# Token-major gate and up products, with the convolution's neighbour rows brought by DMA copies

## The chip, the cores and the metric

The kernel runs on one core of a Trainium2 chip. A core has TensorE (PE, matrix products; its weight loads are listed as PEld), VectorE (DVE), ScalarE (ACT), GpSimd (POOL) and SyncE (SP, which here only issues transfers), each with a queue of its own that it works through in order, and 16 DMA engines. SBUF is the on-chip memory of 128 partitions, PSUM the memory into which PE writes. The metric is the time on the device in microseconds (us); lower is better.

## The reference, cut to what matters

One layer over 256 tokens of width 2048: a normalised input goes through two token mixers, whose merged result is added to x; then comes a gated MLP with a causal convolution of three taps over the tokens, and a last normalisation. The change lies in the MLP (D_FF = 5632):

```python
h = rmsnorm(x, norm_ffn_w[l])
gate, up = jnp.split(jnp.einsum('bsd,df->bsf', h, w_up[l]), 2, axis=-1)
gate = causal_dwconv(gate, conv_ffn_w[l]) + conv_ffn_b[l]   # y[t] = g[t-2] w0 + g[t-1] w1 + g[t] w2
x = x + jnp.einsum('bsf,fd->bsd', jax.nn.gelu(gate, approximate=False) * up, w_down[l])
return rmsnorm(x, norm_final_w)
```

The convolution is taken for each of the 5632 channels alone, over the tokens. Everything is float32.

## The kernel before, in words

Products are formed from pairs of numbers: each float32 operand is split into a high part in the fp32r format and a low part, the rest. A product is hi·hi + lo·hi + hi·lo.

**Weights.** `srcs` lists all weights tiles in the order of use, 256 rows by 512 columns each, 512 KB. `begin` (L104) loads one on SP's queue into `raw` (four buffers, L109), ACT casts it to `whi` (L111), and DVE takes the rest as `wlo` (L118); `whi` and `wlo` have three buffers each. `weights()` keeps three tiles begun, the one in use and two ahead. A `raw` buffer is free for the next load when its `wlo` is made, a `whi` or `wlo` buffer when PE has used it.

**Two forms of a product.** `gemm_a` (L137) has the tokens on PSUM's partitions: for each of the two rows of 128 in a weights tile and each half of the tokens (t) it issues three matmuls of 512 columns (L148 to L150), twelve per tile; the stationary operand is a 128x128 block of the activations, the weights stream. Its result is `[128 tokens, 2, 512 channels]`, two PSUM banks from the pool `psm`, which has two such buffers. At the second tile it runs whatever waits in the list `later`. `gemm_b` (L156) has the channels on the partitions: the weights are stationary, and 512 columns stream past, the high part of all 256 tokens beside the low part (L172); a second matmul of 256 columns takes the weights' low part (L173). That is 16 matmuls per tile, and four results `[128 channels, 2, 256]` that come by turns from `psm` and from `psg` (four buffers of one bank). `merged` (L177) adds the two halves: ACT copies one out (L181), DVE adds (L182).

**The mixers** (to 777 us) use `gemm_a`; their results are evicted by ACT with the norm's factor as a scale (L449) and turned by `turned` (L185), eight transposes on PE against the identity (L193). One part of them (`gdn`) sends small matrices through DRAM: `cd` to `cdd`, `cdd` to `lb` (L553, L556), and DVE reads `lb` at L565.

**The MLP** (L794 to L823) has eleven chunks of 512 channels. Each has a gate product and an up product of eight weights tiles. The gate's result is merged, multiplied with the norm's factor `rb2` (one value per token, broadcast over the partitions at L303), and convolved: the tokens are on the free axis, so that a neighbour is a shifted slice (L804 and eight instructions at L808), with the taps as one value per partition (`cfw`, `vec`, turned at L268 and L278 at the kernel's start). Then come Gelu on ACT (L810), a multiplication with `rb2` on POOL (L811), the multiplication with the up product (L813), and the split in `hhi` and `hlo` (L820, L821), which are the stationary operands of the down projection.

**The down projection** (L841 to L850) holds its result in eight banks at once, four column groups (c) by two halves of the tokens, and goes through 22 pairs of rows; for each pair and c it takes one weights tile and twelve matmuls (L836 to L838).

**The order** on each queue is laid out when the program is built, by a planner that estimates how long each instruction and transfer takes and lets the earliest ready one go first; at run time each engine goes through its queue in that order and waits at an instruction until its inputs are there.

Of the kernel before, what the change touches and what calls it, by code (L numbers as in the profile page):

```python
# [7 lines left out]
F32 = mybir.dt.float32  # L8
# [5 lines left out]
P = 128  # L14
S = 256
# [7 lines left out]
PAD = 16  # L23
NB = 128 + PAD + 128
# [9 lines left out]
def kernel(  # L34
# [59 lines left out]
    srcs += [down[c][kp] for kp in range(KF // 2) for c in range(4)]  # L94
# [58 lines left out]

    banks = [0]

    def gemm_b(rhl, nk):  # L156

        banks[0] ^= 1  # L160
        if banks[0]:
            pair = [pm(), pm()]
            ps = [pair[f // 2][:, f % 2].rearrange("p (a s) -> p a s", a=2) for f in range(4)]
        else:
            ps = [pg([P, 2, S]) for f in range(4)]
        for c in range(nk // 2):
            hi, lo = weights()
            for f in range(4):
                fs = slice(f * P, (f + 1) * P)
                for kk in range(2):  # L170
                    k = 2 * c + kk
                    mm(ps[f], hi[:, kk, fs], rhl(k), start=(k == 0), stop=False, skip_group_check=True)  # L172
                    mm(ps[f][:, 1, :], lo[:, kk, fs], rhl(k)[:, 0, :], start=False, stop=(k == nk - 1),  # L173
                       skip_group_check=True)
        return ps

    def merged(ps, dst):  # L177

        for f in range(4):
            low_half = fp.tile([P, S], F32, tag="lh", bufs=3, name=nm("lh"))  # L180
            nc.scalar.copy(low_half, ps[f][:, 1, :])  # L181
            nc.vector.tensor_tensor(dst[:, f, :], ps[f][:, 0, :], low_half, op=ALU.add)  # L182
        return dst
# [66 lines left out]
    NV = 16 + KF  # L250
    V_FFN, V_CB = 0, 16
    vrows = mp.tile([NV, P], F32, tag="th", name="vrows")
    for off, n, src in ((V_FFN, 16, norm_ffn_w), (V_CB, KF, conv_ffn_b)):
        nc.scalar.dma_start(vrows[off : off + n, :], src[0].rearrange("(r p) -> r p", p=P))
    cqrows = mp.tile([96, 2, P], F32, tag="cy", bufs=2, name="cqrows")
    nc.scalar.dma_start(cqrows, conv_qkv_w.rearrange("o j (r p) -> (o j r) p", p=P)
                        .rearrange("(a q) p -> q a p", a=2))
    cfrows = mp.tile([66, 2, P], F32, tag="cy", bufs=2, name="cfrows")
    nc.scalar.dma_start(cfrows, conv_ffn_w.rearrange("o j (r p) -> (o j r) p", p=P)
# [6 lines left out]
    vec = cpool.tile([P, NV], F32, name="vec")  # L266
    pv = pg()
    nc.tensor.transpose(pv[:, :NV], vrows, ident[:NV, :NV])  # L268
    nc.vector.tensor_copy(vec, pv[:, :NV])
# [20 lines left out]
    def rstd_rows(ssq, dst):  # L290
# [6 lines left out]
        if dst is None:  # L297
            return rs
        pr = pg()
        for t in range(2):  # L300
            dg = cpool.tile([P, P], F32, tag="diag", bufs=2, name=nm("diag"))
            nc.vector.tensor_scalar(dg, ident, rs[:, t : t + 1], None, op0=ALU.mult)
            mm(pr[:, t * P : (t + 1) * P], ones, dg, start=True, stop=True)  # L303
        nc.vector.tensor_copy(dst, pr[:, :S])
        return rs
# [8 lines left out]
    rs1 = rstd_rows(ssq, None)  # L314
# [454 lines left out]
    for c in range(4):  # L769
        ps = gemm_a(at(mhi), at(mlo), KD)  # L770
        xs = xt[:, :, c * 512 : (c + 1) * 512]
        nc.vector.tensor_tensor(xs, xs, ps, op=ALU.add)
        for t in range(2):
            jk = cpool.tile([P, 512], F32, tag="sqj", name=nm("sqj"))
            nc.scalar.activation(jk, xs[:, t, :], AF.Square, accum_out=ssq4[:, t, c : c + 1])
        for k2 in range(2):
            pt = pg([P, 2, S])
            for kk in range(2):
                k = 4 * c + 2 * k2 + kk
                for t in range(2):  # L780
                    nc.tensor.transpose(pt[:, kk, t * P : (t + 1) * P], xt[:, t, k * P : (k + 1) * P], ident)
            for kk in range(2):
                k = 4 * c + 2 * k2 + kk
                nw = vec[:, V_FFN + k : V_FFN + k + 1]
# [11 lines left out]
    rb2b = rb2.unsqueeze(1).to_broadcast([P, 4, S])  # L796
    for c in range(DFF // 512):
        ps = gemm_b(lambda k: fhl[:, k], KD)
        gs = fp.tile([P, 4, S], F32, tag="gs", bufs=2, name=nm("gs"))
        nc.vector.tensor_tensor(gs, merged(ps, gs), rb2b, op=ALU.mult)  # L800
        y = fp.tile([P, 4, S], F32, tag="y", name=nm("y"))
        for f in range(4):
            r = 4 * c + f
            nc.vector.tensor_scalar(y[:, f, :], gs[:, f, :], cfw[:, 2 * KF + r : 2 * KF + r + 1],  # L804
                                    vec[:, V_CB + r : V_CB + r + 1], op0=ALU.mult, op1=ALU.add)
            for j in (1, 0):
                s = 2 - j
                nc.vector.scalar_tensor_tensor(y[:, f, s:], gs[:, f, : S - s], cfw[:, j * KF + r : j * KF + r + 1],  # L808
                                               y[:, f, s:], op0=ALU.mult, op1=ALU.add)
        nc.scalar.activation(y, y, AF.Gelu)  # L810
        nc.gpsimd.tensor_tensor(y, y, rb2b, op=ALU.mult)  # L811
# [15 lines left out]
    acc = [[pg() for t in range(2)] for c in range(2)]  # L827
    for c in range(2):
        ps = pm()
        acc.append([ps[:, t, :] for t in range(2)])  # L830
# [10 lines left out]
    for kp in range(LAST + 1):  # L841
# [60 lines left out]
```

## Time and profile before

| | |
|---|---|
| median of three runs | 1593.93 us (1593.29 to 1594.85) |
| the profiled execution | 1594.1 us |
| its span, first to last instruction | 1592.3 us |
| TensorE's granted clock over the span | 0.998 |
| busy: PE, PEld, DVE, ACT, POOL | 98%, 83%, 67%, 47%, 7% |
| busy share of the DMA engines, transferred | 60.8% on SP's queue, 0.8% on ACT's; 291.62 MB |

The span is what the profile counts from the first to the last instruction; the run's own time has the start and the end beside it. Busy shares are means over stages that have different limits. In a group of instructions the columns are line, engine, operation, result and operands with their shapes, count, then busy time in us and the mean of one in ns, then the idle time of the engine ahead of them and what ended it. In a timeline the columns are start, duration, engine, line, operation; square brackets give the idle time ahead of it and who ended it. PE's matmuls overlap, so a duration of 0.39 us says less than the distance from one start to the next. The queue q1 is SP's and q10 is ACT's; their columns are packets, MB, and the share of the 16 engines' time.

### The profile page before, as it was taken

How to read it: one execution, taken by the hardware profiler on the slowest of the kernel's cores; microseconds unless marked ns; L12 is line 12 of the kernel's file. 1: busy time of each engine (PE TensorE's matmuls, PEld its weight loads, DVE VectorE, ACT ScalarE, POOL GpSimd, SP SyncE). 2: the span in 40 equal slices, each digit the busy share in tenths (PEclk: the TensorE clock that was granted, in tenths of full speed). 3: DMA queues.
4: the chain of work that ended last, by engine and by line, in shares of the span. 5: the costliest groups of instructions: out<-in, count | busy, mean ns of one | idle time of the engine just before them, and what ended most of it. 6: DMA issues, size and time to landing. Idle time of an engine off the chain costs nothing.

```text
span 1592.3 us, 21435 instructions
## 1 busy us (share of the span) xinstructions
PE 1568.1 (98%) x8116; PEld 1317.5 (83%) x8116; DVE 1066.7 (67%) x1624; ACT 750.1 (47%) x969; POOL 115.7 (7%) x132
## 2 busy tenths in 40 slices
PE   8999999999999999999999999999999999999997
PEld 6878888888888888887788888888888888888886
DVE  6778758786778757786555777666666677444445
ACT  6455435544455445544454544444444444333334
POOL 3020100110020100102000000000000000000000
PEclk9999999999999999999999999999999999999999
DMA  7656656566556656665556666666666666656563
GB/s 251 185 153 191 193 144 179 168 189 176 159 152 189 198 145 177 170 191 162 200 184 182 187 187 192 190 186 187 185 195 186 187 191 209 201 191 197 191 193 132
DMA packets 159789, 291.62 MB, mean 183 GB/s; under 512 B 17974, under 2 KB 21062, under 8 KB 159302
## 3 DMA queue, kind: packets, MB, share of 16 engines
q1 hardware_dynamic: 157792, 285.77, 60.8%
q10 hardware_dynamic: 1894, 4.48, 0.8%
q8 instruction: 63, 1.03, 0.3%
q14 instruction: 40, 0.33, 0.1%
HBM read 287.07 MB, written 3.15 MB: 182 GB/s over the span
## 4 chain that ended last, share of the span: by engine, by line
PE 89%; DVE 3%; DMA 3%; issue 3%; POOL 2%; SPq 1%; ACT 0%; DVEq 0%; POOLq 0%
PE psm L150 12%; PE psm L149 12%; PE psm L148 12%; PE psm L172 10%; PE psg L172 10%; PE psg L173 5%; PE psm L173 5%; PE psg L836 3%; PE psg L838 3%; PE psg L837 3%; PE psm L838 2%; PE psm L836 2%; PE psm L837 2%; DVE wlo L118 1%; PE psg L518 1%
## 5 line engine op out<-in xcount | busy, mean ns | idle before, releaser
L118 DVE TENSOR_TENSOR wlo<-raw,whi 128x1024 fp32r<-128x1024 f32 x528 | 657.8, 1247 | 414.1 <-ACT whi L111 407.8
L111 ACT CAST whi<-raw 128x1024 fp32r<-128x1024 f32 x530 | 557.8, 1053 | 753.7 <-PE psm L149 331.4
L150 PE MATMUL psm<-wlo,xhl 128*128 128x512 f32 x896 | 352.9, 394 | 2.7 <-DVE wlo L118 2.7
L148 PE MATMUL psm<-whi,xhl 128*128 128x512 f32 x896 | 352.1, 393 | 1.9 <-ACT xhl L237 1.9
L149 PE MATMUL psm<-whi,xhl 128*128 128x512 f32 x896 | 351.9, 393 | 0.0
L172 PE MATMUL psm<-fhl,whi 128*128 128x512 f32 x704 | 245.9, 396 | 0.0
L172 PE MATMUL psg<-fhl,whi 128*128 128x512 f32 x704 | 237.8, 394 | 0.0
L150 PEld LDWEIGHTS psm<-wlo,xhl 128*128 128x128 f32 x896 | 168.6, 188 | 38.4 <-DVE wlo L118 4.3
L148 PEld LDWEIGHTS psm<-whi,xhl 128*128 128x128 f32 x896 | 168.7, 188 | 35.9 <-ACT xhl L237 2.3
L149 PEld LDWEIGHTS psm<-whi,xhl 128*128 128x128 f32 x896 | 168.6, 188 | 34.7
L173 PE MATMUL psm<-fhl,wlo 128*128 128x256 f32 x704 | 194.2, 279 | 0.0
L173 PE MATMUL psg<-fhl,wlo 128*128 128x256 f32 x704 | 178.6, 279 | 0.0
L172 PEld LDWEIGHTS psm<-fhl,whi 128*128 128x128 f32 x704 | 131.3, 188 | 30.4
L172 PEld LDWEIGHTS psg<-fhl,whi 128*128 128x128 f32 x704 | 129.2, 188 | 24.0
L173 PEld LDWEIGHTS psg<-fhl,wlo 128*128 128x128 f32 x704 | 132.4, 188 | 6.9
L173 PEld LDWEIGHTS psm<-fhl,wlo 128*128 128x128 f32 x704 | 132.5, 188 | 1.1
L836 PE MATMUL psg<-whi,hhi 128*128 128x512 f32 x176 | 68.6, 390 | 0.0
L836 PE MATMUL psm<-whi,hhi 128*128 128x512 f32 x176 | 68.5, 389 | 0.0
L837 PE MATMUL psm<-whi,hlo 128*128 128x512 f32 x176 | 68.5, 389 | 0.0
L837 PE MATMUL psg<-whi,hlo 128*128 128x512 f32 x176 | 68.5, 389 | 0.0
L838 PE MATMUL psm<-wlo,hhi 128*128 128x512 f32 x176 | 68.5, 389 | 0.0
L838 PE MATMUL psg<-wlo,hhi 128*128 128x512 f32 x176 | 61.7, 389 | 0.0
(233 smaller groups left out, 1515.3 us busy)
## 6 DMA issues: line engine op xcount, KB each, us to landing
raw<-in_w_in_dram SPq DMA_DIRECT2D x226, 512.0 KB, 3.8
raw<-in_w_up_dram SPq DMA_DIRECT2D x176, 512.0 KB, 3.9
raw<-in_w_down_dram SPq DMA_DIRECT2D x88, 512.0 KB, 3.9
raw<-in_w_out_dram SPq DMA_DIRECT2D x32, 512.0 KB, 3.6
raw<-in_pool_w_dram SPq DMA_DIRECT2D x8, 512.0 KB, 3.9
x<-in_x_dram SPq DMA_DIRECT2D x4, 512.0 KB, 8.5
lb<-cdd SPq DMA_DIRECT2D x16, 128.0 KB, 2.7
xt<-in_x_dram ACTq DMA_DIRECT2D x1, 2048.0 KB, 8.3
```

The costliest lines, as they stand in the source:

```text
L111: nc.scalar.copy(hi, raw)
L118: nc.vector.tensor_tensor(lo, raw, hi.bitcast(F32), op=ALU.subtract)
L148: mm(ps[:, t, :], lh(k, t), hi[:, kk, :], start=(k == 0), stop=False)
L149: mm(ps[:, t, :], ll(k, t), hi[:, kk, :], start=False, stop=False)
L150: mm(ps[:, t, :], lh(k, t), lo[:, kk, :], start=False, stop=(k == nk - 1))
L172: mm(ps[f], hi[:, kk, fs], rhl(k), start=(k == 0), stop=False, skip_group_check=True)
L173: mm(ps[f][:, 1, :], lo[:, kk, fs], rhl(k)[:, 0, :], start=False, stop=(k == nk - 1), skip_group_check=True)
L518: mm(pg0, kq[:, h, 0, 0:P], kq[:, h, :, :], start=True, stop=True)
L836: mm(acc[c][t], lh(k, t), hi[:, kk, :], start=(k == 0), stop=False)
L837: mm(acc[c][t], ll(k, t), hi[:, kk, :], start=False, stop=False)
L838: mm(acc[c][t], lh(k, t), lo[:, kk, :], start=False, stop=(k == KF - 1))
```

## The change

The gate and up products use `gemm_a`, as the mixers do, so that tokens are on the partitions and channels on the free axis; `gemm_b`, `merged` and the broadcast factor `rb2` go. ACT evicts the gate with the norm's factor as its scale into `gt` `[128, 2, 512]`. A token's neighbours then lie on other partitions: for j = 1 and j = 2, a copy on ACT's DMA queue moves the rows of `gt` on by j partitions into `moved[j-1]` (128 - j rows of 4 KB), and a second one brings the j rows that go from the first half of the tokens to the second. The taps and the bias come by four broadcast transfers per chunk on SP's queue, one row of 512 values to all partitions.

`gate_conv` (run at the up product's second tile) multiplies `gt` and the two moved copies with their taps, adds the bias and the copies, and applies Gelu; the up product is multiplied in from PSUM with the norm's factor. `hidden` (run at the next product's second tile) turns the result with eight transposes and splits it. `gt` and `taps` have one buffer each.

In the down projection, the first round goes through the column groups in the order 1, 2, 3, 0, and the last chunk's `hidden` is run in it before group 2; PSUM is taken group by group.

```diff
+FIRST_DOWN = (1, 2, 3, 0)
...
-    srcs += [down[c][kp] for kp in range(KF // 2) for c in range(4)]
+    srcs += [down[c][kp] for kp in range(KF // 2) for c in (range(4) if kp else FIRST_DOWN)]
...
-    def gemm_b(rhl, nk):
...
-    def merged(ps, dst):
...
-    cfw = cpool.tile([P, 132], F32, name="cfw")
-    pv = pg()
-    for a in range(2):
-        nc.tensor.transpose(pv[:, a * 66 : (a + 1) * 66], cfrows[:, a, :], ident[:66, :66])
-    nc.vector.tensor_copy(cfw, pv[:, :132])
...
-    rb2 = cpool.tile([P, S], F32, tag="rb", name="rb2")
-    rstd_rows(ssq2, rb2)
+    rs2 = rstd_rows(ssq2)
...
+    moved = [fp.tile([P, 2, 512], F32, name=f"mv{j}") for j in (1, 2)]
+    for j in (1, 2):
+        nc.gpsimd.memset(moved[j - 1][0:j, 0, :], 0.0)
+
+    def gate_conv(gt, taps):
+
+        for m, j in ((gt, 2), (moved[0], 1), (moved[1], 0)):
+            nc.vector.tensor_tensor(m, m, taps[:, j, :].unsqueeze(1).to_broadcast([P, 2, 512]), op=ALU.mult)
+        nc.vector.tensor_tensor(gt, gt, taps[:, 3, :].unsqueeze(1).to_broadcast([P, 2, 512]), op=ALU.add)
+        for m in moved:
+            nc.vector.tensor_tensor(gt, gt, m, op=ALU.add)
+        nc.scalar.activation(gt, gt, AF.Gelu)
+
+    def hidden(gt, hh, hl):
+        for f2, pt in enumerate(turned(gt)):
+            fs = slice(2 * f2, 2 * f2 + 2)
+            nc.scalar.copy(hh[:, fs, :], pt)
+            nc.vector.tensor_tensor(hl[:, fs, :], pt, hh[:, fs, :].bitcast(F32), op=ALU.subtract)
+
     for c in range(DFF // 512):
-        ps = gemm_b(lambda k: fhl[:, k], KD)
-        gs = fp.tile([P, 4, S], F32, tag="gs", bufs=2, name=nm("gs"))
-        nc.vector.tensor_tensor(gs, merged(ps, gs), rb2b, op=ALU.mult)
...
-        ps = gemm_b(lambda k: fhl[:, k], KD)
-        nc.vector.tensor_tensor(gs, merged(ps, gs), y, op=ALU.mult)
+        ps = gemm_a(fh, fl, KD)
+        gt = fp.tile([P, 2, 512], F32, tag="gs", name=nm("gs"))
+        for t in range(2):
+            nc.scalar.activation(gt[:, t, :], ps[:, t, :], AF.Copy, scale=rs2[:, t : t + 1])
+        for j in (1, 2):
+            nc.scalar.dma_start(moved[j - 1][j:P], gt[0 : P - j])
+            nc.scalar.dma_start(moved[j - 1][0:j, 1, :], gt[P - j : P, 0, :])
+        taps = fp.tile([P, 4, 512], F32, tag="taps", name=nm("taps"))
+        for j in range(3):
+            nc.sync.dma_start(taps[:, j, :], conv_ffn_w[0, j, 512 * c : 512 * c + 512].partition_broadcast(P))
+        nc.sync.dma_start(taps[:, 3, :], conv_ffn_b[0, 512 * c : 512 * c + 512].partition_broadcast(P))
+        later.append(lambda gt=gt, taps=taps: gate_conv(gt, taps))
+        ps = gemm_a(fh, fl, KD)
+        for t in range(2):
+            nc.vector.scalar_tensor_tensor(gt[:, t, :], ps[:, t, :], rs2[:, t : t + 1], gt[:, t, :],
+                                           op0=ALU.mult, op1=ALU.mult)
...
-        nc.scalar.copy(hh, gs)
-        nc.vector.tensor_tensor(hl, gs, hh.bitcast(F32), op=ALU.subtract)
+        later.append(lambda gt=gt, hh=hh, hl=hl: hidden(gt, hh, hl))
...
-    for kp in range(LAST + 1):
+    for c in FIRST_DOWN:
+        if c == 2:
+            while later:
+                later.pop(0)()
...
+        w = weights()
+        for t in range(2):
+            down_part(0, c, t, *w)
+    for kp in range(1, LAST + 1):
```

More of the change, by code (lines that the diff above doesn't have):

```diff
@@ L152, in gemm_a @@
         return ps
-    banks = [0]
-    def gemm_b(rhl, nk):
[L160 to L175, printed above, removed]
-    def merged(ps, dst):
[L179 to L183, printed above, removed]
     def turned(src):
@@ L247 @@
     ps_k0 = gemm_a(xh, xl, KD)
[L250 to L254, printed above, removed]
+    vrows = mp.tile([KD, P], F32, tag="th", name="vrows")
+    nc.scalar.dma_start(vrows, norm_ffn_w[0].rearrange("(r p) -> r p", p=P))
     cqrows = mp.tile([96, 2, P], F32, tag="cy", bufs=2, name="cqrows")
     nc.scalar.dma_start(cqrows, conv_qkv_w.rearrange("o j (r p) -> (o j r) p", p=P)
[L257 to L259 removed]
                         .rearrange("(a q) p -> q a p", a=2))
@@ L264 @@
     nc.scalar.dma_start(dtb, dt_bias[0].partition_broadcast(P))
-    vec = cpool.tile([P, NV], F32, name="vec")
+    vec = cpool.tile([P, KD], F32, name="vec")
     pv = pg()
-    nc.tensor.transpose(pv[:, :NV], vrows, ident[:NV, :NV])
-    nc.vector.tensor_copy(vec, pv[:, :NV])
+    nc.tensor.transpose(pv[:, :KD], vrows, ident[:KD, :KD])
+    nc.vector.tensor_copy(vec, pv[:, :KD])
     cqw = cpool.tile([P, 192], F32, name="cqw")
@@ L296, in rstd_rows @@
         nc.gpsimd.tensor_tensor(rs, ms, epsx, op=ALU.pow)
[L297 to L304, printed above, removed]
         return rs
@@ L313 @@
     nc.vector.tensor_reduce(ssq, ssq4, axis=mybir.AxisListType.X, op=ALU.add)
[L314 removed]
+    rs1 = rstd_rows(ssq)
     rsh = cpool.tile([P, 2], F32, name="rsh")
@@ L826 @@
     nc.scalar.dma_start(nfin, norm_final_w.partition_broadcast(P))
[L827 to L830, printed above, removed]
+    acc = [None] * 4
     lh, ll = at(hhi), at(hlo)
@@ L840 @@
     LAST = KF // 2 - 1
-    for kp in range(LAST + 1):
+    for c in FIRST_DOWN:
+        if c == 2:
+            while later:
+                later.pop(0)()
+        if c < 2:
+            acc[c] = [pg() for t in range(2)]
+        else:
+            ps = pm()
+            acc[c] = [ps[:, t, :] for t in range(2)]
+        w = weights()
+        for t in range(2):
+            down_part(0, c, t, *w)
+    for kp in range(1, LAST + 1):
         for c in range(4 if kp < LAST else 1):
```

20 lines of the change are left out of this document (6 added, 14 removed).

## The prediction

> **What bounds the kernel now.** I read the page's head first, then the table by stretches, for one 512-column chunk of the gate and up products (columns: start and end, length, then busy time and count for PE, PEld, DVE, ACT, POOL, then granted clock, DMA share, GB/s); the last row is a stretch in which the DMA engines have hardly a pause.
>
> ```profile
> span 1592.3 us, 21435 instructions
> 928.85:973.54 44.69, 44.69 (x257) 39.01 (x257) 30.51 (x40) 21.42 (x27) 2.49 (x1) 1.00 0.65 189
> 10.00:20.00 10.00, 9.23 (x43) 7.89 (x42) 8.78 (x21) 8.60 (x22) 1.33 (x4) 1.00 0.95 345
> ```
>
> A chunk takes 44.69 us, and TensorE (PE) has no gap in it; DVE works 30.5 us of it, ACT 21.4. So PE's own pace bounds this stage, and anything that makes PE wait is added in full. The timeline gives that pace, now for L172/L173 and, in the down projection, for the three-matmul order that the change takes over:
>
> ```profile
> 1000.05 0.39 PE L172 MATMUL psm<-fhl,whi 128*128 128x512 f32 x1
> 1002.82 0.39 PE L172 MATMUL psm<-fhl,whi 128*128 128x512 f32 x1
> 1402.16 0.39 PE L836 MATMUL psm<-whi,hhi 128*128 128x512 f32 x1
> 1404.88 0.39 PE L836 MATMUL psm<-whi,hhi 128*128 128x512 f32 x1
> 776.58 0.39 PE L150 MATMUL psm<-wlo,mhi 128*128 128x512 f32 x1
> 776.90 1.06 PE L193 MATMUL psg<-ident,sz 128*128 128x128 f32 x8
> 777.89 0.50 PE L148 MATMUL psm<-whi,mhi 128*128 128x512 f32 x1
> ```
>
> One weights tile (16 matmuls, eight pairs) takes 2.77 us now; twelve matmuls of 512 columns take 2.72 us. Eight transposes push the next product from 0.23 us after its forerunner to 1.31 us: 1.08 us.
>
> PE is fed by ACT (hi half, L111) and DVE (lo half, L118), two tiles ahead. Where DVE meets a wait, this breaks:
>
> ```profile
> L118 DVE TENSOR_TENSOR wlo<-raw,whi 128x1024 fp32r<-128x1024 f32 x528 | 657.8, 1247 | 414.1 <-ACT whi L111 407.8
> L111 ACT CAST whi<-raw 128x1024 fp32r<-128x1024 f32 x530 | 557.8, 1053 | 753.7 <-PE psm L149 331.4
> DVE tmp L565 <- DMA lb<-cdd: 12.7, 4, 3.9
> 302.91 0.42 DVE L565 TENSOR_TENSOR tmp<-lb,tb 128x248 f32<-128x248 f32 x1 [3.13 <-DMA lb<-cdd]
> 305.29 0.50 PE L150 MATMUL psm<-wlo,xhl 128*128 128x512 f32 x1 [0.20 <-DVE wlo L118]
> 486.76 0.42 DVE L565 TENSOR_TENSOR tmp<-lb,tb 128x248 f32<-128x248 f32 x1 [3.66 <-DMA lb<-cdd]
> 489.14 0.50 PE L150 MATMUL psm<-wlo,xhl 128*128 128x512 f32 x1 [0.73 <-DVE wlo L118]
> ```
>
> At the four places where DVE first reads lb, which came by DMA, it stands up to 3.9 us (third row: total, times, longest): the planner had put the reader ahead of the landing. PE then waits for the wlo queued behind it: 3.13 us of DVE give 0.20 us of PE, 3.66 give 0.73. So about 2.93 us of a DVE stall are covered, the rest is paid.
>
> **The change part by part.** *Products.* 22 products of eight tiles at 2.72 us: 43.52 us a chunk, against 44.69; with the eight transposes 44.60 at 1.08 us, 44.51 if only the 0.99 us from their start to the next product count. I take the second, 0.18 us saved a chunk, 2 us in all (bounds 1 and 2).
>
> *Arithmetic on DVE and ACT.*
>
> ```profile
> L449 ACT ACTIVATE ev<-psm,rs 128x512 f32<-128x512 f32 x30 | 18.9, 681 | 1.6 <-PE psm L150 1.6
> L742 DVE TENSOR_TENSOR sz<-sz,yb 128x1024 f32<-128x1024 f32 x4 | 4.9, 1225 | 0.1
> L717 DVE TENSOR_TENSOR plo<-psg,phi 128x512 fp32r<-128x512 f32 x8 | 5.5, 684 | 0.0
> ...
> raw<-in_w_up_dram SPq DMA_DIRECT2D x176, 512.0 KB, 3.9
> ```
>
> DVE per chunk: 16 wlo at 1.25, six passes of the convolution at 1.23, four half passes from PSUM at about 0.7: 30 us, as now. ACT: 16 whi, two evictions at 0.68, Gelu, two casts: about 20.5, as now, and four DMA issues more, behind which a whi stands with the 2.93 us found above to spare. POOL loses its 2.5 us. Work alone costs nothing; its cover is the 14 us a chunk in which DVE idles. What goes once (L278's transposes, the row broadcast of the norm's factor at L303, its copy) stands beside products and is costed at nothing; uncovered it would be a handful of short instructions, once.
>
> *Bias and taps.* Four broadcasts of 256 KB a chunk on SP's queue, between the weights. Their tile is free once the previous chunk's convolution has read it, so they come a chunk early. 1 MB at 345 GB/s is 3.0 us in which the weights behind them are late. A raw tile is asked for four tiles before its use: 10.9 us, less 2.3 for hi and lo and 3.9 to land (last row), 4.7 to spare. SP waits at the taps for the previous convolution's last use of them, with weights behind it; these wait for lo halves that come later still. Cost nothing; 11 x 3.0 us without that cover.
>
> *The moved rows.* This is the term that decides. Per chunk ACT's queue gets a copy of 127 rows of 4 KB (one row on), one of 126 (two on) and two scraps. How does a transfer spread over the 16 DMA engines? The queue's rows, with every transfer ACT issues now (KB each, us to landing); first the stretch that holds only xt's:
>
> ```profile
> q10 hardware_dynamic: 272, 2.10, 56.9%
> xt<-in_x_dram ACTq DMA_DIRECT2D x1, 2048.0 KB, 8.3
> ...
> q10 hardware_dynamic: 1894, 4.48, 0.8%
> lb<-cdd SPq DMA_DIRECT2D x16, 128.0 KB, 2.7
> psb<-in_pool_scale_dram ACTq DMA_DIRECT2D x4, 256.0 KB, 4.2
> nfin<-in_norm_final_w_dram ACTq DMA_DIRECT2D x1, 1024.0 KB
> cqrows<-in_conv_qkv_w_dram ACTq DMA_DIRECT2D x1, 96.0 KB, 7.3
> cfrows<-in_conv_ffn_w_dram ACTq DMA_DIRECT2D x1, 66.0 KB
> gwb<-in_gdn_norm_w_dram ACTq DMA_DIRECT2D x1, 64.0 KB, 7.8
> vrows<-in_conv_ffn_b_dram ACTq DMA_DIRECT2D x1, 22.0 KB
> nmrows<-in_norm_mix_w_dram ACTq DMA_DIRECT2D x1, 8.0 KB, 2.8
> vrows<-in_norm_ffn_w_dram ACTq DMA_DIRECT2D x1, 8.0 KB, 5.2
> alb<-in_a_log_dram ACTq DMA_DIRECT2D x1, 8.0 KB, 6.5
> dtb<-in_dt_bias_dram ACTq DMA_DIRECT2D x1, 8.0 KB
> ```
>
> xt is 256 rows of 8 KB and leaves 272 packets: 16 more, one per engine. In the whole run, 14 transfers have 256 (xt) + 128 (nfin) + 4 x 128 (psb) + 192 + 132 (cqrows, cfrows) + 128 (gwb) + 44 + 16 (vrows) + 16 (nmrows) + 2 x 128 (alb, dtb) = 1680 packets of data. 1894 - 1680 = 214 closing ones, ten short of 14 x 16. Two transfers have rows that 16 doesn't divide, 44 and 66; at 11 engines each, the largest divisor up to 16, exactly ten are missing. Rows handed out in equal lots as far as they go would make it 15 and 14, three missing. So the engines used divide the row count. 126 gives 14. 127 is prime: one engine for 520,192 bytes.
>
> The Trainium skill, "DMA: Bandwidth & Descriptors", section "Why a DMA increments its semaphore by 16 and not by 1", says the same and names the case: 127 partitions go on one engine. By it the sum is mine; by sixteen engines it would be the second rival's.
>
> One engine's pace: 345/16/0.95 = 22.7 GB/s where all are full, 189/16/0.65 = 18.2 in this stage: 22.9 or 28.6 us. Ahead of that 2.3 us that lb needs beyond its 0.4 us of data; behind it perhaps the second copy's nine rows on that engine, 1.6 us. Landing 25.2 to 32.5 us after issue, and I take 28.9, the middle, since two or three weights tiles share the engine. The issue comes two evictions (1.4 us) after the gate product ends (T).
>
> Who waits: in gate_conv, the first multiply overwrites gt, so it waits for all copies that read it. Behind it on DVE: lo halves; behind these PE. The rows on lb say that the planner allows a transfer a few us, so I put the multiply in the queue at about T + 5, where the lo halves of the up product's tiles 0 to 3 are made and tile 4's is not: tile 3's buffer is free when tile 0 is used up, T + 2.72, and hi and lo take 2.3, so T + 5.0. PE stops at tile 4's third matmul, T + 4 x 2.72 + 0.45 = T + 11.3. It goes on when copy, one or two multiplies and a wlo are done: T + 1.4 + 28.9 + 3.0 = T + 33.3. Stall 22.0 us a chunk; 17.8 at the early end; 29 at the late end with tile 3's lo behind it too. Afterwards the up product (four tiles, 11 us) still covers Gelu (1.05 us), so nothing else is late; the transposes wait for nothing new.
>
> After such a pause PE is slow at first. The timeline at the kernel's start:
>
> ```profile
> 10.85 1.97 PE L233 MATMUL psg<-ident,x 128*128 128x128 f32 x8 [0.77 <-DMA x<-in_x_dram]
> 13.47 0.63 PE L148 MATMUL psm<-whi,xhl 128*128 128x512 f32 x1
> 13.90 0.63 PE L149 MATMUL psm<-whi,xhl 128*128 128x512 f32 x1
> 14.65 0.39 PE L148 MATMUL psm<-whi,xhl 128*128 128x512 f32 x1
> 14.88 0.39 PE L149 MATMUL psm<-whi,xhl 128*128 128x512 f32 x1
> ```
>
> Starts are 0.43 us apart, later 0.23. From 10.85, when PE began to work with hardly a pause, to about 14.5 it ran at half pace, which cost 1.8 us. Bounds 0 and 1.8; I take 1.8, as the pauses are long.
>
> *Down projection's first round.* In the order 1, 2, 3, 0 the last chunk's eight transposes follow twelve products of column group 1 (2.72 us), while DVE forms the chunk; group 0 takes the PSUM buffers that the transposes leave. Cost nothing beyond the transposes, which are in the sum; uncovered 2.7 us once.
>
> Sum: 1592.3 - 2 + 11 x (22.0 + 1.8) = 1852 us of span; the profiled execution is 1594.1, 1.8 above its span and 0.2 above the median. 1854 us, +16%. Own range: 11 x 17.8 - 3 gives 1787, 11 x 30.8 - 1 gives 1932.
>
> **The rivals.** *The planner knows that the copy is long* and queues the multiplies behind the up product's lo halves. Then DVE doesn't stand, and the one engine is the bound: 16 weights tiles x 32 KB, taps 64 KB, 508 and 36 KB of moved rows make 1.147 MB a chunk, 50.5 us at 22.7 GB/s, 63 at 18.2. Against 44.69 that is 11 x 5.8 or 11 x 18.3 more, so 1658 to 1796, likeliest near 1670. Against it: the four waits on lb. For it: nothing shown here has few engines for much data.
>
> *Not slower.* The copies spread over all engines: 1.03 MB at 345 to 156 GB/s (345 less the stage's 189) plus 2.3 lands 5.3 to 8.9 us after issue. The price is DVE's wait less 2.93 us; it decides at 3.1 us of waiting, where the 0.18 us saved are used up. With less: 1592 to 1593. With a wait of 5: 11 x 2.1, 1615. Against it: the 214 packets.
>
> *Still slower.* A copy with both ends in SBUF may go at half that pace; no row has one with large rows. Then 45.8 us of data, a stall near 40 us, and 1594 + 11 x 42 = 2056. For it: nothing but that the kind is missing.
>
> **How the numbers follow.** Forecast 0.62, rival one 0.20, rival two 0.10 (half of it slower), rival three 0.08. The range 1655 to 1932 leaves out rival two, rival three and a little of the first. The likeliest case alone: 1787 to 1932. A measurement of this kernel can tell 0.2%. Faster 0.02, same 0.03, slower 0.95.
>
> **What would show it.** Right: eleven idle stretches of PE of some 20 us, released by wlo, with DVE waiting for the moved rows; the copy of 508 KB landing after 25 us or more; each chunk's products near 43.5 us beside the stall; packets beyond the data that are few for that copy. Wrong: moved rows that land within 10 us, multiplies queued late on DVE, or PE without gaps as before.

## The result and the profile after

The changed kernel takes 1852.41 us, the median of five runs (1851.75 to 1856.68), against 1593.93 us: 1.1626 times the time before, 95% interval 1.1613 to 1.1639. The profiled execution took 1852.25 us. Lines of code have moved a little: the hi half is made at L112, the lo half at L119, the products' three matmuls stand at L149, L150 and L151, the gate tile is evicted at L774, the large copies are issued at L776, the scraps at L777, and the convolution multiplies at L758.

The page of the changed kernel: the span, PE's row, the granted clock in 40 slices, ACT's DMA queue, the chain that ended last, and the convolution's multiplies.

```profile
span 1850.2 us, 20069 instructions
PE 1603.9 (87%) x7494; PEld 1313.7 (71%) x7494; DVE 1043.8 (56%) x1477; ACT 732.1 (40%) x914; POOL 88.2 (5%) x123
PEclk9999999999999999999779779779779879899999
q10 hardware_dynamic: 5040, 15.86, 2.4%
PE 73%; DMA 17%; DVE 3%; issue 3%; ACT 2%; POOL 1%; SPq 0%; DVEq 0%; POOLq 0%; ACTq 0%
L758 DVE TENSOR_TENSOR mv<-mv,taps 128x1024 f32<-128x1024 f32 x22 | 26.9, 1222 | 275.0 <-DMA mv<-gs 275.0
```

PE was busy 98% of the span and is now busy 87%. The clock row dips only from the middle on, where the eleven chunks lie. The chain has 17% of DMA. The last row says which: the multiplies stood 275.0 us, 25.0 a chunk, until the moved rows had landed.

Ten chunks in the table by stretches (start and end, length, busy time and count of PE, PEld, DVE, ACT and POOL, granted clock, DMA share, GB/s), and the waits of the same kernel (us in total, times, longest):

```profile
887.52:1570.13 682.61, 480.66 (x2001) 387.17 (x2001) 286.62 (x260) 199.48 (x212) 0.00 (x0) 0.83 0.50 154
```

```profile
DVE mv L758 <- DMA mv<-gs: 275.0, 11, 25.4
ACT whi L112 <- issue: 153.0, 20, 13.6
PE psm L151 <- DVE wlo L119: 139.5, 18, 13.5
PE psm L149 <- ACT whi L112: 86.4, 12, 8.6
```

A chunk takes 682.61 / 10 = 68.3 us in place of 44.69. PE stops twice in each: about 7.8 us (86.4 / 11) for a hi half and about 12.4 for a lo half (136.3 of the 139.5, over 11; the rest are seven short waits ahead of the chunks, which the kernel without copies has as well), 20.2 in all. Of the rest of the 23.7 lost per chunk (counted below against the run without copies) most is PE at half pace after each stop. The second row is new in its size: ACT stands some 13 us a chunk in its own issuing, where its longest such wait in the kernel before was 1.5 us.

One chunk, from the timeline of the changed kernel (start, duration, engine, line, operation, and in brackets the idle time ahead and who ended it); ACT first, then DVE, then PE:

```profile
1008.22 1.26 ACT L774 ACTIVATE gs<-psm,rs 128x512 f32<-128x512 f32 x2
1008.93 0.56 ACTq L777 DMA_DIRECT2D mv<-gs  x1
1009.53 9.93 ACTq L776 DMA_DIRECT2D mv<-gs  x2
1019.50 3.17 ACTq L777 DMA_DIRECT2D mv<-gs  x1
```

```profile
1034.67 1.22 DVE L758 TENSOR_TENSOR mv<-mv,taps 128x1024 f32<-128x1024 f32 x1 [25.09 <-DMA mv<-gs]
```

```profile
1023.88 0.80 PE L149 MATMUL psm<-whi,fhl 128*128 128x512 f32 x1 [8.27 <-ACT whi L112]
...
1037.08 0.79 PE L151 MATMUL psm<-wlo,fhl 128*128 128x512 f32 x1 [11.97 <-DVE wlo L119]
...
1041.94 0.63 PE L150 MATMUL psm<-whi,fhl 128*128 128x512 f32 x1
1042.37 0.48 PE L151 MATMUL psm<-wlo,fhl 128*128 128x512 f32 x1
1042.68 0.40 PE L149 MATMUL psm<-whi,fhl 128*128 128x512 f32 x1
```

The two large copies are issued at 1009.5 and 1010.2, and the second issue lasts until 1019.5. Only then does ACT get to the scrap and, at 1022.8, to the next hi halves, so PE stops first for ACT. It does two matmuls and stops again, for the lo half that stands on DVE behind the multiply. The multiply begins at 1034.67, 25.1 us after the first of the two issues. PE goes on at 1037.08, and its starts lie 0.43 us apart until 1042.4, 5.3 us long; later they lie 0.23 apart.

### The profile page after: what moved, and what is told of

Same layout as the page of the kernel before. It is cut to its first block, busy times and chain, and to the rows that moved or that the text cites. A ratio compares the mean times of both kernels' runs of the same rounds, so it can differ in the third digit from the quotient of the medians.

```text
span 1850.2 us, 20069 instructions
## 1 busy us (share of the span) xinstructions
PE 1603.9 (87%) x7494; PEld 1313.7 (71%) x7494; DVE 1043.8 (56%) x1477; ACT 732.1 (40%) x914; POOL 88.2 (5%) x123
## 3 DMA queue, kind: packets, MB, share of 16 engines
q1 hardware_dynamic: 164128, 297.31, 53.9%
q10 hardware_dynamic: 5040, 15.86, 2.4%
## 4 chain that ended last, share of the span: by engine, by line
PE 73%; DMA 17%; DVE 3%; issue 3%; ACT 2%; POOL 1%; SPq 0%; DVEq 0%; POOLq 0%; ACTq 0%
PE psm L151 18%; PE psm L150 18%; PE psm L149 18%; DMA mv<-gs 15%; PE psg L806 2%; PE psg L807 2%; PE psg L805 2%; PE psm L806 2%; PE psm L805 2%; PE psm L807 2%; DVE wlo L119 2%; PE psg L163 1%; ACT whi L112 1%; PE psg L468 1%; ACT gs L774 1%
## 5 line engine op out<-in xcount | busy, mean ns | idle before, releaser
L112 ACT CAST whi<-raw 128x1024 fp32r<-128x1024 f32 x530 | 555.3, 1052 | 1036.7 <-PE psm L150 718.2
L119 DVE TENSOR_TENSOR wlo<-raw,whi 128x1024 fp32r<-128x1024 f32 x528 | 649.9, 1234 | 408.9 <-ACT whi L112 398.0
L151 PE MATMUL psm<-wlo,fhl 128*128 128x512 f32 x704 | 286.8, 410 | 136.3 <-DVE wlo L119 136.3
L149 PE MATMUL psm<-whi,fhl 128*128 128x512 f32 x704 | 289.9, 412 | 85.5 <-ACT whi L112 85.5
L151 PE MATMUL psm<-wlo,xhl 128*128 128x512 f32 x896 | 352.9, 394 | 2.5 <-DVE wlo L119 2.5
L149 PE MATMUL psm<-whi,xhl 128*128 128x512 f32 x896 | 352.1, 393 | 1.9 <-ACT xhl L207 1.9
L150 PE MATMUL psm<-whi,xhl 128*128 128x512 f32 x896 | 351.7, 393 | 0.0
L150 PE MATMUL psm<-whi,fhl 128*128 128x512 f32 x704 | 287.2, 408 | 0.0
L151 PEld LDWEIGHTS psm<-wlo,fhl 128*128 128x128 f32 x704 | 139.4, 198 | 173.4 <-DVE wlo L119 144.2
L149 PEld LDWEIGHTS psm<-whi,fhl 128*128 128x128 f32 x704 | 140.5, 200 | 118.7 <-ACT whi L112 90.1
L151 PEld LDWEIGHTS psm<-wlo,xhl 128*128 128x128 f32 x896 | 168.5, 188 | 38.0 <-DVE wlo L119 3.9
L149 PEld LDWEIGHTS psm<-whi,xhl 128*128 128x128 f32 x896 | 168.8, 188 | 36.0 <-ACT xhl L207 2.3
L150 PEld LDWEIGHTS psm<-whi,xhl 128*128 128x128 f32 x896 | 168.6, 188 | 34.5
L758 DVE TENSOR_TENSOR mv<-mv,taps 128x1024 f32<-128x1024 f32 x22 | 26.9, 1222 | 275.0 <-DMA mv<-gs 275.0
L150 PEld LDWEIGHTS psm<-whi,fhl 128*128 128x128 f32 x704 | 140.1, 199 | 29.7
L416 DVE SCALAR_TENSOR_TENSOR cy<-psg,cqw,cy 128x255 f32<-128x255 f32 (+1 forms) x144 | 60.5, 472 | 0.4 <-ACT cy L413 0.4
```

The costliest lines, as they stand in the source:

```text
L112: nc.scalar.copy(hi, raw)
L119: nc.vector.tensor_tensor(lo, raw, hi.bitcast(F32), op=ALU.subtract)
L149: mm(ps[:, t, :], lh(k, t), hi[:, kk, :], start=(k == 0), stop=False)
L150: mm(ps[:, t, :], ll(k, t), hi[:, kk, :], start=False, stop=False)
L151: mm(ps[:, t, :], lh(k, t), lo[:, kk, :], start=False, stop=(k == nk - 1))
L416: nc.vector.scalar_tensor_tensor(y[:, f, s:], gs[:, : S - s], w(j), y[:, f, s:], op0=ALU.mult, op1=ALU.add)
```

## The experiments

All use the changed kernel as their base. In the end each loss is counted per chunk against the run without the copies (1591.33 us): the time less 1591.33, over 11.

**1. The 127 rows cut into 126 and 1.** If the prime number of rows puts the copy on one engine, cutting off one row removes nearly all of the loss.

```diff
-            nc.scalar.dma_start(moved[j - 1][j:P], gt[0 : P - j])
+            nc.scalar.dma_start(moved[j - 1][j : 126 + j], gt[0:126])
+            if j == 1:
+                nc.scalar.dma_start(moved[0][127:128], gt[126:127])
```

> The 127-row copy is cut into one of 126 rows and one of a single row; nothing else changes. Theory one (a copy of 127 rows goes on one DMA engine, its late landing is the whole loss): 126 rows go on 14 engines, the moved rows land 6 to 9 us after issue, PE's waits per chunk fall from 20 us to under 3, the time to 1592 to 1625 us. Rival A (large copies from SBUF to SBUF are slow on any number of engines): landing stays above 20 us and the time near 1850. Rival B (ACT is held by the issue of a copy with many rows, whatever the engines): ACT still stands some 10 us per chunk, time near 1680.

Measured: 1603.37 us (1600.26 to 1604.35), ratio to before 1.0056, interval 1.0039 to 1.0073. One row cut off takes 249 us away. From the timeline of this kernel, ACT after the eviction, and from its waits:

```profile
1009.56 0.54 ACTq L779 DMA_DIRECT2D mv<-gs  x1
...
1011.60 1.62 ACTq L776 DMA_DIRECT2D mv<-gs  x1
1013.26 0.63 ACTq L779 DMA_DIRECT2D mv<-gs  x1
```

```profile
PE psm L151 <- DVE wlo L119: 8.5, 12, 2.1
DVE mv L758 <- DMA mv<-gs: 7.0, 5, 2.7
```

The long issue is gone (the first of five issues begins at 1009.56, the last ends at 1013.89, 4.3 us, and the longest takes 1.62), and so is the wait for the rows: 7.0 us in the whole run. Both rivals of this expectation fall. So does the prediction's second rival (the copies spread) for the changed kernel; its first (DVE doesn't stand) is not tested here, but fell with the 275.0 us above.

**2. All four copies issued by SP.** Does ACT's standing add to the time, or does it lie inside the wait for the rows?

```diff
-            nc.scalar.dma_start(moved[j - 1][j:P], gt[0 : P - j])
-            nc.scalar.dma_start(moved[j - 1][0:j, 1, :], gt[P - j : P, 0, :])
+            nc.sync.dma_start(moved[j - 1][j:P], gt[0 : P - j])
+            nc.sync.dma_start(moved[j - 1][0:j, 1, :], gt[P - j : P, 0, :])
```

> The four copies of the changed kernel are issued by SP and not by ACT; rows as they were. Theory one: the landing decides; PE stops at the third matmul of the third tile (waiting for wlo) and not at its first (waiting for whi), and goes on at the same moment: 1840 to 1860 us. Theory two (ACT's standing during the issue, after which PE waits 8.3 us for whi, is a loss of its own that adds to the landing): 11 x 8.3 less, about 1760. In both SP itself stands during the issue, and weights behind it come late; if these are what PE waits for, more than 1860.

Measured: 1816.64 us, in one execution: under the 1840 to 1860 of the first theory, far above the 1760 of the second. The waits of this kernel, then the issue of the two large copies and the multiply in one chunk:

```profile
ACT whi L112 <- DMA raw<-in_w_up_dram: 245.0, 27, 21.0
DVE mv L758 <- DMA mv<-gs: 240.7, 11, 22.3
PE psm L151 <- DVE wlo L119: 198.3, 17, 18.2
```

```profile
1004.97 8.77 SPq L776 DMA_DIRECT2D mv<-gs  x2
1029.41 1.22 DVE L758 TENSOR_TENSOR mv<-mv,taps 128x1024 f32<-128x1024 f32 x1 [21.68 <-DMA mv<-gs]
```

PE now stops once a chunk, about 17.8 us (195.8 of the 198.3 lie in the eleven chunks), for wlo alone; the stop for whi has gone into it. From the issue to the multiply it is 24.4 us in this chunk, hardly less than the 25.1 of the changed kernel. What is shorter is DVE's wait, 21.9 us a chunk in place of 25.0: DVE first makes one more lo half and comes to the multiply 2.8 us after the issue (1029.41 - 21.68 - 1004.97), while in the changed kernel it stood there as soon as the copy was issued. So the 36 us less, 3.3 a chunk, are 2.4 of shorter stop (20.2 less 17.8) and 0.9 less beyond the stop.

**3. The copies made, but waited for by nobody.** The convolution writes a tile of its own from the chunk's own rows; the copies stay on ACT.

```diff
-        for m, j in ((gt, 2), (moved[0], 1), (moved[1], 0)):
-            nc.vector.tensor_tensor(m, m, taps[:, j, :].unsqueeze(1).to_broadcast([P, 2, 512]), op=ALU.mult)
+        for d, m, j in ((y, gt, 2), (y, y, 1), (y, y, 0)):
+            nc.vector.tensor_tensor(d, m, taps[:, j, :].unsqueeze(1).to_broadcast([P, 2, 512]), op=ALU.mult)
```

> The copies stay, of 127 and 126 rows, on ACT's queue, but nobody waits for them: the convolution writes a tile of its own and uses the chunk's own rows in place of the moved ones (as many DVE passes, neighbours' terms left out). What remains is ACT standing at the issue and the load on one DMA engine. If the landing is the only loss: 1592 to 1600 us. If ACT's standing costs by itself: the 8.3 us of PE waiting for whi stay, with 2 to 3 us of slow clock behind, 1592 + 11 x (8 to 11), 1680 to 1715. If the one engine's load holds up the weights: more than that.

Measured: 1769.18 us, in one execution, more than both of the first two cases. The waits of this kernel:

```profile
ACT whi L112 <- issue: 150.8, 20, 13.3
ACT whi L112 <- DMA raw<-in_w_up_dram: 122.2, 40, 8.7
PE psm L149 <- ACT whi L112: 118.1, 22, 8.2
```

Without any wait for the rows 178 us remain, 16.2 a chunk. Two candidates stand in the first two rows: ACT at the issue, and weights that land late. Experiments 9 and 12 tell them apart.

**4. No copies at all.** This is the floor, and it prices everything in the change but the copies.

```diff
-        for j in (1, 2):
-            nc.scalar.dma_start(moved[j - 1][j:P], gt[0 : P - j])
-            nc.scalar.dma_start(moved[j - 1][0:j, 1, :], gt[P - j : P, 0, :])
```

> No copies at all; the moved tiles hold zeros (the neighbours' terms are left out), all DVE passes, the taps' broadcasts and the rest of the change stay. It gives what the change is worth without its copies. The sum of the prediction's other terms: 2 us less than before, 1590 to 1593 us. If the tokens-on-partitions form, the taps' transfers or the hidden transposes cost something by themselves: above 1597.

Measured: 1591.33 us, ratio 0.999, interval 0.9981 to 0.9999. So the rest of the change is worth about 2 us, and the whole loss of 261 us belongs to the copies.

**5. All four copies issued by POOL.** Is the one engine a matter of the rows alone, or of the queue as well?

```diff
-            nc.scalar.dma_start(moved[j - 1][j:P], gt[0 : P - j])
-            nc.scalar.dma_start(moved[j - 1][0:j, 1, :], gt[P - j : P, 0, :])
+            nc.gpsimd.dma_start(moved[j - 1][j:P], gt[0 : P - j])
+            nc.gpsimd.dma_start(moved[j - 1][0:j, 1, :], gt[P - j : P, 0, :])
```

> The four copies of each chunk are issued by POOL in place of ACT, nothing else is changed. Theory one (the rows of a copy fix how many DMA engines it takes, whoever issues it): the 127 rows still take one engine for about 21 us, ACT no longer stands 13 us at the issue, the multiply still waits some 22 to 25 us for the copy; 1780 to 1850 us, like the run with the copies on SP. Rival (the one engine belongs to the queue of ACT and SP, not to the rows): POOL's queue spreads the 127 rows, the multiply waits under 3 us, 1592 to 1615 us.

Measured: 1591.06 us (1589.72 to 1594.55), ratio 0.9992, interval 0.9981 to 1.0002. My theory said 1780 to 1850 and was wrong; the rival was right. From the page of this kernel (POOL's queue, ACT's queue, the issue of the same 508 KB with its median time to land) and its waits:

```profile
q0 software_dynamic: 3872, 11.47, 2.9%
q10 hardware_dynamic: 1696, 4.39, 0.8%
mv<-gs POOLq DMA_DIRECT2D x11, 508.0 KB, 5.9
```

```profile
DVE mv L758 <- DMA mv<-gs: 14.9, 11, 3.0
```

The very same 127 rows land in 5.9 us from POOL's queue. The multiply waits 1.4 us a chunk, and PE's lead of two tiles hides that. ACT's queue has 1696 packets left without the copies, so in the changed kernel (5040) the copies of a chunk made (5040 - 1696) / 11 = 304 packets there; here they make 3872 / 11 = 352. The data are the same 271 packets in the traces of both: 127, 126 and 2 rows, and 16 for the scrap of one row, which goes in pieces of 128 bytes. The rest are closing ones, 33 a chunk on ACT's queue (1 + 14 + 2 + 16, as the rule of the divisors has it for 127, 126 and 2 rows and 16 pieces) and 81 on POOL's. That the rows are spread is seen directly: in this kernel's trace the packets of the two large copies overlap and all 253 are through in 6 us, while on ACT's queue the packets of the 127 rows follow one another without overlap. The Trainium skill, "DMA: Bandwidth & Descriptors", section "Why a DMA increments its semaphore by 16 and not by 1", has this as an exception to its rule: a copy issued by GpSimd can get all sixteen engines with the partitions dealt out in nearly equal lots, 127 among them. The landing of 5.9 us agrees. The Trainium skill, "DMA: Bandwidth & Descriptors", section "Issuing engines are not separate DMA queues", says that starting DMAs from several engines saves only the time of issuing them. Moving these copies from ACT to POOL was worth 261 us, more than the 153 us that ACT stood at its issues, so for a row count like 127 the measurement decides against that sentence.

**6 and 7. The cut of experiment 1, issued by POOL, and by SP.** Where do the 10 us of experiment 1 go?

```diff
-            nc.scalar.dma_start(moved[j - 1][j : 126 + j], gt[0:126])
+            nc.gpsimd.dma_start(moved[j - 1][j : 126 + j], gt[0:126])
```

(and so on for the others; `nc.sync` in the second)

> The 127-row copy cut into 126 rows and 1 row as before, and all five copies issued by POOL. Theory one for the 10 us that the cut version is still over the kernel before: ACT stands 4.3 us per chunk in issuing (five issues of 0.5 to 1.6 us), and the whi and wlo behind it are late; without it the time is 1590 to 1596 us. Rival: the 10 us come from the copies themselves, which hold up the weights' loads or the multiplies that wait for them; then it stays at 1599 to 1605 us.

> The same cut, all five copies issued by SP. Theory one: ACT is free, but SP stands until the gate tile is evicted, with the loads of the weights queued behind it; the loads run several tiles ahead, so 1590 to 1600 us. Rival (the copies themselves hold up the loads): 1599 to 1610 us with waits for raw in the row of whi.

Measured: 1591.87 us on POOL (ratio 0.9992, interval 0.9983 to 1.0002) and 1595.7 us on SP (1.0014, 1.0004 to 1.0023). With ACT free of the five issues the 10 us are gone on POOL, and all but some 3 on SP. So most of them came from ACT's 4.3 us of issuing per chunk and not from the copies; what the rest on SP is, no run shows. A cheap issue is not free on an engine that PE's lead hangs on.

**8. A smaller dose: 61 rows on one engine.** 61 is prime; 66 has the divisor 11.

```diff
+            if j == 1:
+                nc.scalar.dma_start(moved[0][1:62], gt[0:61])
+                nc.scalar.dma_start(moved[0][62:128], gt[61:127])
+            else:
+                nc.scalar.dma_start(moved[1][2:128], gt[0:126])
```

> A smaller dose: the 127 rows cut into 61 rows (a prime number, so one engine by the rule of theory one) and 66 rows (eleven engines); all on ACT. Theory one: the 61 rows hold one engine for 61/127 of the time, about 10 us in place of 21; the multiply waits some 5 to 12 us in place of 25, the PE, which in the changed kernel stands still from about T+5.4 on, loses 0 to 8 us per chunk; 1605 to 1690 us. If the loss were in proportion to the rows on the one engine it would be 1593 + 259 x 61/127 = 1717 us. Rival (any copy of a shape that does not divide costs the whole wait, whatever its rows): 1800 us and more. Rival (61 rows are spread, the rule is another one): 1600 to 1607 us like the cut at 126.

Measured: 1740.24 us (1739.8 to 1741.95), ratio 1.0926, interval 1.091 to 1.0943. This is above my range and outside both rivals' ranges. From this kernel's page, its waits and its timeline (ACT's first large issue, then DVE and PE of the same chunk):

```profile
q10 hardware_dynamic: 5161, 15.86, 2.9%
```

```profile
PE psm L151 <- DVE wlo L119: 122.2, 17, 11.5
```

```profile
989.59 0.64 ACTq L777 DMA_DIRECT2D mv<-gs  x1
1006.90 1.22 DVE L758 TENSOR_TENSOR mv<-mv,taps 128x1024 f32<-128x1024 f32 x1 [11.87 <-DMA mv<-gs]
1009.31 0.79 PE L151 MATMUL psm<-wlo,fhl 128*128 128x512 f32 x1 [10.46 <-DVE wlo L119]
```

The mechanism holds: (5161 - 5040) / 11 = 11 packets a chunk more than in the changed kernel, so the same 127 rows have twelve closing packets in place of one, as one engine for 61 rows and eleven for 66 would give. There is no long issue on ACT, and one stop a chunk, for the rows. The size doesn't: 13.5 us are lost per chunk, and I had said 0 to 8. I had taken 10 us for the data; the multiply came 17.3 us after the issue, since the rows shared their engine with the weights (in the trace 4 to 6 of them come per us while weights' packets stand between them). From 61 to 127 rows the loss grows by 23.7 - 13.5 = 10.2 us, 0.155 us a row; in the trace the one engine's packets of 4096 bytes take about 0.16 us each. So each of the 66 further rows on the one engine is paid in full, one after the other.

**9. 61 rows, waited for by nobody.** The cut of 8 in the kernel of 3.

> The cut at 61 and 66 rows, and nobody waits for the copies (the convolution uses the chunk's own rows, as in the run where the copies were not read; the neighbours' terms are left out). In the run with the 127 rows not read 16 us per chunk were lost though nobody waited. Theory one: they are lost because ACT stands about 13 us at the issue of a copy behind the 127 rows; at 61 rows ACT stands about 3 us, so 1592 to 1615 us. Rival: they are lost because the one engine that carries the rows holds up the weights' loads, a part of which it carries as well; then the loss goes with the rows, 1593 + 176 x 61/127 = 1678 us, 1650 to 1700.

Measured: 1680.69 us, ratio 1.0549 (1.0519 to 1.058), against 1592 to 1615 by my theory and 1678 by the rival. The waits of this kernel:

```profile
ACT whi L112 <- DMA raw<-in_w_up_dram: 130.3, 32, 10.8
PE psm L149 <- ACT whi L112: 61.4, 11, 6.7
```

ACT no longer stands at an issue. It waits for weights, up to 10.8 us for one tile: each weights tile has a part on every engine and has landed only when the loaded engine has brought its part too.

**10. The 126 rows issued ahead of the 127.**

```diff
-        for j in (1, 2):
+        for j in (2, 1):
```

> The changed kernel with the loop over the two copies turned, so that ACT issues the 126 rows ahead of the 127. Theory one (the long issue is that of the copy that comes behind the 127 rows and is held until that one engine has worked off most of them): the 126 rows' issue no longer stands 9 us, ACT stands under 6 us per chunk and makes the whi in time; the multiply still waits about 22 to 25 us for the 127 rows and the PE stops once per chunk in place of twice, for wlo; 1810 to 1850 us, as with the copies on SP (1817). Rival (the two stops add up, and ACT's part goes): 1593 + 11 x (12 + 2) = 1750 us, 1730 to 1780.

Measured: 1852.32 us, ratio 1.1626 (1.1585 to 1.1668): no change. ACT in the timeline of this kernel:

```profile
1011.85 1.50 ACTq L776 DMA_DIRECT2D mv<-gs  x2
1013.38 10.75 ACTq L777 DMA_DIRECT2D mv<-gs  x1
1024.25 2.94 ACT L112 CAST whi<-raw 128x1024 fp32r<-128x1024 f32 x3 [12.53 <-issue]
```

Both large issues now take 1.50 us together, and it is the scrap behind them, 2 or 4 KB, that lasts 10.75 us. So it is the next issue behind the 127 rows that stands, whatever it carries. In the traces it ends, in every chunk, when 40 to 46 of the 127 rows have set out, here (not counting the 126), in the changed kernel and on SP (2). It looks as if 81 to 87 rows could still be waiting when the next issue goes through, which would fit that nothing stands behind 61 rows (8); no run tried a count between, and why it stands stays open. I had expected ACT to be free with that; it stands 12.5 us as before, and neither 1810 to 1850 nor 1730 to 1780 came out.

**11. The 127 rows alone on ACT, nothing issued behind them.** The 126 rows and the scraps go to POOL.

```diff
-            nc.scalar.dma_start(moved[j - 1][j:P], gt[0 : P - j])
-            nc.scalar.dma_start(moved[j - 1][0:j, 1, :], gt[P - j : P, 0, :])
+            (nc.scalar if j == 1 else nc.gpsimd).dma_start(moved[j - 1][j:P], gt[0 : P - j])
+            nc.gpsimd.dma_start(moved[j - 1][0:j, 1, :], gt[P - j : P, 0, :])
```

> The 127-row copy alone stays with ACT, whose queue holds nothing behind it; the 126 rows and the two scraps are issued by POOL. Theory one (the multiply's wait for the 127 rows sets the time, and ACT's standing at the issue of the copy behind them lies inside that wait): ACT stands under 2 us, the PE stops once per chunk, for wlo, 18 to 20 us; 1800 to 1830 us, as with the copies on SP (1817). Rival (ACT's standing adds its own 8 us to the wait): 1593 + 11 x (12.3 + 2) = 1750 us.

Measured: 1852.96 us, ratio 1.1618 (1.1584 to 1.1652). From the page, the waits and the timeline of this kernel (ACT, DVE, PE):

```profile
q10 hardware_dynamic: 3104, 10.11, 1.4%
```

```profile
PE psm L151 <- DVE wlo L119: 239.8, 18, 22.0
```

```profile
1008.27 1.26 ACT L774 ACTIVATE gs<-psm,rs 128x512 f32<-128x512 f32 x2
1009.56 0.63 ACTq L776 DMA_DIRECT2D mv<-gs  x1
1038.40 1.22 DVE L758 TENSOR_TENSOR mv<-mv,taps 128x1024 f32<-128x1024 f32 x1 [25.80 <-DMA mv<-gs]
1040.82 0.79 PE L151 MATMUL psm<-wlo,fhl 128*128 128x512 f32 x1 [21.98 <-DVE wlo L119]
```

This settles two things. The count: (3104 - 1696) / 11 = 128 packets a chunk, 127 rows and exactly one closing packet, so one engine. In the trace these packets follow one another without overlap. And ACT's standing: it is gone (the issue takes 0.63 us), PE stops once, 21.98 us in this chunk, and the time is that of the changed kernel, somewhat above the 1800 to 1830 I had expected. The standing lies inside the wait for the rows. The rows take 28.8 us from issue to multiply here, 3.7 more than in the changed kernel: ACT works on, so the weights' loads go on and share the engine (in the trace the rows' packets come 3 to 4 per us at first, 6 to 7 later; from 4 to 26 us after the issue one weights tile of 512 KB goes through here, and hardly any of the weights in the changed kernel, where the rows come 6 to 7 per us from the first on).

**12. The same, waited for by nobody.**

> The same, and nobody waits for the copies (own rows used, the neighbours' terms left out). ACT's standing is gone and so is the wait; what is left is that one engine carries 127 rows beside its part of the weights' loads. If that load alone makes the loss of the run in which the 127 rows were not read (176 us), it stays: 8.0 us per chunk at 61 rows x 127/61 = 16.6 us, 1776 us, 1750 to 1790. If half of it was ACT's standing (8.1 us per chunk in that run's waits): about 1680 us. If the loads run far enough ahead at that: 1592 to 1610 us.

Measured: 1782.49 us, ratio 1.1176 (1.1144 to 1.1209); the first forecast, from the 61 rows in proportion, was 1776. The waits of this kernel:

```profile
ACT whi L112 <- DMA raw<-in_w_up_dram: 265.2, 59, 11.1
PE psm L149 <- ACT whi L112: 119.0, 22, 6.7
```

No engine stands at an issue, none waits for the rows, and 17.4 us a chunk are lost all the same, to weights that land late behind the one engine. The trace shows the sharing: from 1013 to 1016 us a row of 4096 bytes (0.16 us) and a weights' packet of 2048 bytes (0.09 us) alternate, one of each at a time, and no other weights' packet moves. With the 61 rows the loss was 8.1.

All in one table:

| run | us | lost per chunk |
|---|---|---|
| no copies (4) | 1591.33 | 0 |
| POOL issues, 127 rows (5); cut, POOL (6) | 1591.06; 1591.87 | 0; 0 |
| cut, SP (7); cut, ACT (1) | 1595.7; 1603.37 | 0.4; 1.1 |
| 61 rows on one engine: not read (9); read (8) | 1680.69; 1740.24 | 8.1; 13.5 |
| 127 rows, not read: on ACT (3); alone (12) | 1769.18; 1782.49 | 16.2; 17.4 |
| 127 rows, read: SP (2); ACT (changed kernel, 10, 11) | 1816.64; 1852.41, 1852.32, 1852.96 | 20.5; 23.7 to 23.8 |

No version with the whole convolution is faster than the kernel before by more than can be told; the two with POOL and the one without copies end at 1591 to 1592, PE's own pace.

## Why the prediction was right, and where it was not

*One engine for the 127 rows* was the step that decides, and it is shown: one row less takes 249 us away (1), the copy alone leaves 128 packets (11), and in the trace these come one at a time. It was drawn from ten missing packets in the queue of the kernel before. What the step left out is its condition: the rule holds for ACT's queue and, by the (167472 - 164128) / 11 = 304 packets a chunk that SP's queue has more with the copies (2) than without (4), for SP's, not for POOL's (5).

*Landing 28.9 us after the issue, the stop at tile 4's third matmul, going on at T + 33.3, a stall of 22.0, 1.8 for the slow clock.* The changed kernel itself shows other parts with the same sum: landing 25.1 us after the issue, just under the earliest of the forecast (25.2), two stops of 7.8 and 12.4 us, and 23.7 - 20.2 = 3.5 us beyond the stops, most of it slow clock, since PE starts slowly after both. Experiment 11, with ACT's standing removed, shows the parts as they were forecast: 28.8 us from issue to multiply, one stop of 21.6 (237.4 of the 239.8 lie in the eleven chunks), and 23.8 - 21.6 = 2.2 beyond it. That the landing agrees to 0.1 us is partly luck: the 2.3 us ahead of the data were taken from lb, and in the traces the first row sets out 3.4 to 4.1 us after the issue (changed kernel and 11).

*"Four DMA issues more, behind which a whi stands with the 2.93 us found above to spare"* is the step that failed. ACT stood 13 us, because an issue behind the 127 rows on the same queue lasts 9 to 11 us, whatever it carries (10); the trace of before had no row that could show it. It cost nothing on balance: where it made whi late it also held back weights' loads, and the rows landed 3.7 us sooner. That the two cancel here is luck of the sizes; the sum was right by that, not by the step.

*The multiply's place* was off by one tile in the changed kernel. Its stop begins at 1023.88 - 8.27 = 1015.61, 7.4 us after the eviction began; in experiment 11 it begins at 1018.84, 10.6 after. The difference is a tile of 2.72 us and two matmuls.

*Products, taps, arithmetic, down projection*: minus 2 us in all by the sum, 0.2 to 3.0 less by the interval measured without the copies (4). No cover failed there.

*The rivals.* The first (DVE never stands) named the right second bound, the one engine's share of the weights, and put 1658 to 1796 on it, likeliest near 1670. Its mechanism measured alone is 1782 (12), so its price was near its slow end. By 12 and 3, where nobody waits at all, a planner that had known of the long copy could have won at most 70 to 83 us of the 261; this is an estimate, no run tried such an order. The second (copies spread, landing 5.3 to 8.9 us after issue, 1592 to 1593) is what happens on POOL's queue: 5.9 us and 1591. The third, half the pace between two places in SBUF, is refuted by 28.8 us of landing: the pace is 4096 bytes in 0.16 us, about 25 GB/s, when the engine has nothing else.

## What to carry to other kernels

Look at the row count of every copy that ACT or SP issues: the prime counts here, 127 and 61, put all rows on one engine, and the price has three parts that hide one another, the reader's wait, the issuing engine's standing behind it, and every other load that has a part on that engine. Taking away one part alone moved the time by 0 to 83 us of 261; one row cut off, or a queue that spreads the rows, removed them together. Count packets beyond the data in the queue's row before a transfer is costed at the bandwidth of sixteen engines.

## What the runs showed of the hardware that I had not expected

- The same copy of 127 rows of 4 KB lands 24 to 29 us after its issue on ACT's queue and 5.9 us on POOL's (changed kernel, 11 and 5).
- An issue behind such a copy on the same queue lasts 9 to 11 us, even for a scrap of 2 or 4 KB (changed kernel, 10). It ends when 40 to 46 of the 127 rows have set out; behind 61 such rows an issue takes 0.6 to 0.9 us (8).
- A copy that nobody waits for costs 17.4 us a chunk through one engine, although a chunk's mean DMA share was 0.65 before (12).
- After a stop of 22 us PE's starts are 0.43 us apart for 4 us and the loss beyond the stop is 2.2 us; with two stops close together it is 3.5 (11, changed kernel).
